# Level masks built later, and the input scaled by a product with a diagonal, in a hybrid HGRN2 / SSD / ConvFFN block

## The chip, the cores and the metric

The kernel runs on one core of a Trainium2 chip. Five engines work side by side, each through its own queue in order: TensorE (PE in the profile, PEld its weight loads), VectorE (DVE), ScalarE (ACT), GpSimd (POOL) and SyncE (SP), which issues most of the loads. They wait for each other by semaphores. The metric is the device time of one execution in microseconds (us), lower is better.

## What is computed

One layer on 512 tokens of width 2048, all in float32. Cut to what matters here:

```python
mod = silu(c) @ w_mod + b_mod                      # 6 parts of 2048
h = rms_norm(x, norm1_w) * (1.0 + scale1) + shift1
proj = h @ w_in                                    # q, f, i, g | z, xbc, dt
o_a = hgrn2_mixer(q_h, f_h, i_h, g_h, ...)         # 8 heads, chunks of 64
o_b = ssd_mixer(z_s, xbc_s, dt_s, ...)             # 4 groups of 4 heads
x = x + gate1 * (concat(o_a, o_b) @ w_out)
h = rms_norm(x, norm2_w) * (1.0 + scale2) + shift2
u = causal_dwconv(h @ ffn_w_up, ...)
x = x + gate2 * ((silu(u_gate) * u_val) @ ffn_w_down)
out = rms_norm(x, final_norm_w)
```

The change touches two places: how `x` is divided by its root mean square and turned (features on the partitions), and when the masks of the HGRN2 mixer are made.

## The kernel before

Every large product is done as three products of rounded parts (L166 to L168): a weight chunk `raw` is loaded (L146, 256 rows by up to 512 columns), ACT rounds it to `whi` (L161), DVE makes the rest `wlo = raw - whi` (L162), and the activations are held in the same way as `hhi` and `hlo`. There are five buffers for `raw`, two for each of `whi` and `wlo`.

**The start.** Four tiles of 128 tokens of `x` are loaded. For each, `x_rstd` squares and sums on ACT (L303), makes the mean (L306) and takes the power -0.5 on POOL (L307). `x_norm` scales the tile on ACT (L310), turns its 16 blocks of 128x128 on PE (L278), four to a bank, and evicts the four banks to `xT`: three by ACT (L282), one by DVE (L284). Meanwhile DVE sums the modulation `silu(c) @ w_mod`: `mod_pair` takes eight loads `m` of 256 rows (L231; they share the five `raw` buffers) and adds 16 rows' products into `macc` (L236, L238). Eight pairs are needed; each gives two blocks of `modT` (L246 to L249), with which `make_h1` makes `hhi` and `hlo` of two blocks (L329 to L331). So the weight products start when pair 0 and `xT` are there.

**The order of the work.** The SSD columns of `w_in` come first, in segments of a few blocks of rows (`SEGMENTS`), as the pairs become ready; between them stands the first value group, `v_group(0)`. A scheduler orders the instructions of each engine by the order of the program, with some work raised in priority; what stands in a queue is then fixed.

**The masks.** HGRN2 works with seven levels of blocks. `level_masks` writes ones to `one8` (DVE, L668) and cuts seven masks of 128x256 bytes out of it by two selects each on POOL (L672, L674), 14 in all. Before, it stands ahead of the segments. The masks are first read in `hgrn_mix`, after `v_group(1)`.

**The SSD mixers.** After the segments, `ssd_mix` of two groups at a time runs in small steps between the products of `v_group(1)` (`small`). Its helper `decay` fetches a table `mm` of head decays by a DMA that POOL issues (L434: one row for all 128 partitions, 256 KB), and DVE adds (L437), clips (L439) and, behind an exponential on ACT (L440), multiplies it (L441). PE turns blocks of `xbc` into small banks `mis` (L449), which DVE reads for `xdt` (L455) and `y` (L456). The pool of `mis` has two banks, so a turn waits until DVE has read the bank of two turns ago.

Of the kernel before, what the change touches and what calls it, by code (L numbers as in the profile page):

```python
# [10 lines left out]
AF = mybir.ActivationFunctionType  # L11
ALU = mybir.AluOpType
PSUM = bass.MemoryType.PSUM

P = 128
S = 512
NT = S // P
# [17 lines left out]
def hybrid_block_kernel(  # L35
# [22 lines left out]
    def nm(s):  # L58
        uid[0] += 1
        return f"{s}_{uid[0]}"  # L60

    def E(dtype=F32, name="e", tag="e"):
        return big.tile([P, 2048], dtype, tag=tag, name=nm(name), bufs={"e": 13, "y": 2, "a": 2}[tag])

    def T(name="t", dtype=F32):
        return tmp.tile([P, 512], dtype, tag="t", name=nm(name))
# [3 lines left out]
    def ACC(name="acc"):  # L70
        if wide[0]:
            wide[0] += 1
            if wide[0] % 8 in (0, 1):
                return MIS(name)
        return psa.tile([P, 512], F32, tag="acc", name=nm(name))

    def MIS(name="mis"):
        return psm.tile([P, 512], F32, tag="mis", name=nm(name))

    def SM(cols, name="s"):  # L80
        return sml.tile([P, cols], F32, tag=f"s{cols}", name=nm(name))

    def CT(shape, name, dtype=F32):
        return cst.tile(shape, dtype, tag=name, name=name)

    V, A, G, PE = nc.vector, nc.scalar, nc.gpsimd, nc.tensor
# [5 lines left out]
    ident = CT([P, P], "ident")  # L92
# [19 lines left out]
    def vec_rows(parts, name, q=nc.gpsimd):  # L112
        rows = T(name + "r")
        r = 0
        for ap, k in parts:
            q.dma_start(out=rows[r:r + k, 0:P], in_=ap)
            r += k
        return rows, r, name
# [8 lines left out]
    def r1(ap):  # L127
        return ap.rearrange("o (r p) -> (o r) p", p=P)
# [143 lines left out]
                      start=True, stop=True)  # L272
        return ps

    def transposed_one(src, dst, k0, t, evac, ps, n=4):

        for j in range(n):
            PE.transpose(out=ps[:, j * P:(j + 1) * P], in_=src[:, (k0 + j) * P:(k0 + j + 1) * P], identity=ident)  # L278
        o = dst.rearrange("p (j s) -> p j s", j=4)[:, k0 % 4:k0 % 4 + n, t * P:(t + 1) * P]
        i = ps[:, 0:n * P].rearrange("p (j s) -> p j s", j=n)  # L280
        if evac % 2:
            A.copy(out=o, in_=i)  # L282
        else:
            V.tensor_copy(out=o, in_=i)  # L284

    def modulate(src, kt, rb, a, sh, hi, lo):
        t = T("hm")
        V.scalar_tensor_tensor(out=t, in0=src, scalar=a, in1=rb, op0=ALU.mult, op1=ALU.mult)
        A.activation(out=hi, in_=t, func=AF.Identity, bias=sh)
        V.scalar_tensor_tensor(out=lo, in0=t, scalar=sh, in1=hi.bitcast(F32), op0=ALU.add, op1=ALU.subtract)  # L290


    xs_ = [E(name="x") for _ in range(NT)]
    xT = [E(name="xT", tag="a" if q == 3 else "e") for q in range(4)]

    def x_load(t):
        nc.sync.dma_start(out=xs_[t], in_=xd[t * P:(t + 1) * P, :])

    xr = {}

    def x_rstd(t):
        ssq = SM(1, "ssq")
        A.activation(out=xbc[t].rearrange("p b s -> p (b s)"), in_=xs_[t], func=AF.Square, accum_out=ssq)  # L303
        ms = SM(1, "ms")
        xr[t] = r = SM(1, "rstd")
        A.activation(out=ms, in_=ssq, func=AF.Copy, scale=1.0 / D, bias=EPS)  # L306
        G.tensor_tensor(out=r, in0=ms, in1=expo[:, 0:1], op=ALU.pow)  # L307

    def x_norm(t):
        A.activation(out=xs_[t], in_=xs_[t], func=AF.Copy, scale=xr[t])  # L310
        for q in range(4):
            transposed_one(xs_[t], xT[q], 4 * q, t, q < 3, ACC())

    hhi = [None] * KT
    hlo = [None] * KT
# [195 lines left out]
    def ov(t):  # L511
        return otile[t // 2].rearrange("p (t f) -> p t f", t=2)[:, t % 2, :]
# [153 lines left out]
    def level_masks():  # L666
        one8 = tmp.tile([P, 256], I8, tag="t", name="one8")
        V.memset(one8, 1)  # L668
        for h in LEVELS:
            nb = P // (2 * h)  # L670
            m = CT([P, 256], f"lm{h}", I8)
            G.affine_select(out=m, in_=one8, pattern=[[0, 4], [-2 * h, nb], [0, h]], base=0,  # L672
                            channel_multiplier=1, compare_op=ALU.is_ge, fill=0.0)
            G.affine_select(out=m, in_=m, pattern=[[0, 4], [2 * h, nb], [0, h]], base=h - 1,  # L674
                            channel_multiplier=-1, compare_op=ALU.is_ge, fill=0.0)
            lmask[h] = m
# [16 lines left out]
    def advance(p, q=8):  # L693

        while steps and steps[0] <= (p, q):
            next(gens[steps.pop(0)[0]], None)

    for t in range(NT):
        x_load(t)
    rows_1 = vec_rows([(r1(b_mod), 96), (r1(norm1_w), 16), (r1(norm2_w), 16)], "p1", nc.sync)  # L700
    for t in range(NT):
        x_rstd(t)
        x_norm(t)
        advance(0, 2 * t + 1)
    p1 = vec_t(*rows_1)
# [1 line left out]
    advance(0, 8)  # L707
    rows_2 = vec_rows([(r1(hgrn_gnorm_w), 8), (r1(ssd_norm_w), 8), (r2(ssd_conv_w), 64), (r1(ssd_conv_b), 16),
                       (hgrn_lb.rearrange("l (r p) -> (l r) p", p=P), 16)], "p2")
    level_masks()  # L710
    seen = set()
    n_piece = 0
    def v_group(grp):
# [6 lines left out]
    for st, k0, k1 in SEGMENTS:  # L720
# [35 lines left out]
        for (_, blocks), ac in zip(sets[st], accs):  # L756
            for b_, a_ in zip(blocks, ac):
                src, d_ = (a_, dtraw) if b_ is None else (a_, xbc[b_[0]][:, b_[1], :])
# [7 lines left out]
            ssd_dt(dtraw)  # L766
        seen.add(st)

    for g in (0, 3, 2, 1):
        waiting.append(ssd_mix(g))  # L770
    v_group(1)
# [12 lines left out]
    for j in range(2):  # L784
# [11 lines left out]
        for t in range(NT):  # L796
            yo = yv(t)[:, j * 512:(j + 1) * 512]
            for i in range(2):
                V.tensor_scalar(out=yo[:, i * 256:(i + 1) * 256], in0=yo[:, i * 256:(i + 1) * 256],
                                scalar1=r[:, 2 * t + i:2 * t + i + 1], scalar2=None, op0=ALU.mult)  # L800
# [18 lines left out]
    for j in range(2):  # L819
# [5 lines left out]
        for t in range(NT):  # L825
            sg = T("gs")
            A.activation(out=sg, in_=accs[t], func=AF.Silu)
            for i in range(4):
                h = 4 * j + i
                o = ov(t)[:, h * P:(h + 1) * P]  # L830
                V.scalar_tensor_tensor(out=o, in0=o, scalar=orstd[:, h, t:t + 1], in1=sg[:, i * P:(i + 1) * P],
                                       op0=ALU.mult, op1=ALU.mult)
# [33 lines left out]
    for n in range(4):  # L866
        accs = feat_group([(512 * n, 512)], [bl(i) for i in range(4)], chunk_src=wout, kts=order[::2], span=(8, 8),
                          rhs=(mhi, mlo), kk_in=True)
        with tc.high_priority(offset=2000 if n == 3 else 0):
            for i in range(4):  # L870
                kt = 4 * n + i
                V.scalar_tensor_tensor(out=x1f(kt), in0=accs[i], scalar=modT[:, 64 + kt:65 + kt], in1=x1f(kt),
                                       op0=ALU.mult, op1=ALU.add)
# [11 lines left out]
    with tc.high_priority(offset=2000):  # L885
        ps = MIS()
# [16 lines left out]
    for i in range(3):  # L903
        rows = T("fr")
        nc.scalar.dma_start(out=rows[0:2 * NF, 0:P], in_=fw[i * 2 * NF:(i + 1) * 2 * NF, :])
        ps = MIS()
# [4 lines left out]
    ps = MIS()  # L911
# [126 lines left out]
```

## Time and profile before

| what | us |
|---|---|
| median of 3 runs | 2513.89 |
| lowest and highest | 2510.45, 2513.9 |
| the profiled execution: its time | 2516.08 |
| the profiled execution: its span | 2514.4 |
| PE busy in the span | 2443.9 |
| DVE busy in the span | 1497.7 |
| mean granted clock of PE | 0.988 |

A row of the timeline reads: start and duration in us, engine, line, operation, what is written `<-` what is read, shape and count, and in brackets the idle time of the engine before it and what ended it. A row of the waits reads: who waits `<-` for whom, us in total, times, longest. A row of a stretch reads: start:end, its length, busy us of PE, PEld, DVE, ACT and POOL with counts, the granted PE clock, the DMA share and GB/s. Names are the program's, buffer numbers left out. The load bandwidth by fortieths of the span shows where loads are dense: about 270 GB/s in the first three, about 110 behind them, and more again between about 0.57 and 1.2 ms.

### The profile page before, as it was taken

The page shows a single profiled execution, that of the slowest core. Times are in us where ns is not written, and L with a number is a line of the kernel's source. Part 1 is how long each engine was busy: PE and PEld are TensorE (multiplying, and loading weights), DVE is VectorE, ACT ScalarE, POOL GpSimd, SP SyncE. Part 2 cuts the span into 40 slices and gives each one's busy share as a digit, 9 for nine tenths or more (in the row PEclk, how much of TensorE's full clock was granted, in tenths as well). Part 3 has the DMA queues.
Part 4 walks back from the last instruction along what each step waited for, and adds up shares of the span by engine and source line. Part 5 has one row for each costly group of instructions (what it writes and reads, how often), then busy time and mean ns, then how long its engine had stood idle before and what let it go on. Part 6 is the DMA issues. An engine that isn't in the chain of part 4 may idle for free.

```text
span 2514.4 us, 29234 instructions
## 1 busy us (share of the span) xinstructions
PE 2443.9 (97%) x11287; PEld 2015.4 (80%) x11287; DVE 1497.7 (60%) x2253; ACT 754.8 (30%) x1035; POOL 54.1 (2%) x66
## 2 busy tenths in 40 slices
PE   6999998999999999999999999999999999999998
PEld 5777877788878777887888888888888888888887
DVE  6884866556767656587636363635454545454557
ACT  6323422221322432332222222222222222232323
POOL 4000000000000000000000000000000000000000
PEclk8999999999999999999999999999999999999999
DMA  8893575335455666466323332333323232323242
GB/s 272 263 280 107 113 125 106 96 109 151 144 159 155 235 198 200 140 203 230 98 95 98 95 101 93 100 94 99 97 96 101 92 101 93 101 93 100 96 130 85
DMA packets 262823, 335.87 MB, mean 134 GB/s; under 512 B 18092, under 2 KB 182524, under 8 KB 261404
## 3 DMA queue, kind: packets, MB, share of 16 engines
q1 hardware_dynamic: 260432, 327.42, 41.5%
q0 software_dynamic: 1568, 4.31, 2.3%
q10 hardware_dynamic: 684, 2.28, 0.3%
q8 instruction: 88, 1.44, 0.2%
q14 instruction: 51, 0.42, 0.0%
HBM read 329.72 MB, written 4.23 MB: 133 GB/s over the span
## 4 chain that ended last, share of the span: by engine, by line
PE 81%; DMA 9%; DVE 7%; ACT 2%; issue 1%; SPq 0%; POOL 0%; ACTq 0%; DVEq 0%; POOLq 0%
PE acc L166 26%; PE acc L168 25%; PE acc L167 25%; DMA m<-in_w_mod_dram 7%; DVE wlo L162 2%; PE mis L547 2%; DVE macc L189 1%; DVE macc L238 1%; DMA raw<-in_w_in_dram 1%; ACT whi L161 1%; DMA x<-in_x_dram 1%; DMA mm<-acrow 0%; PE mis L201 0%; PE mis L487 0%; POOL rstd L265 0%
## 5 line engine op out<-in xcount | busy, mean ns | idle before, releaser
L162 DVE TENSOR_TENSOR wlo<-raw,whi 128x1024 fp32r<-128x1024 f32 (+1 forms) x408 | 490.4, 1203 | 744.9 <-ACT whi L161 739.3
L161 ACT CAST whi<-raw 128x1024 fp32r<-128x1024 f32 (+2 forms) x416 | 424.3, 1021 | 1403.3 <-PE acc L167 596.5
L166 PE MATMUL acc<-hhi,whi 128*128 128x512 f32 x1920 | 770.0, 402 | 11.7 <-ACT whi L161 7.1
L168 PE MATMUL acc<-hhi,wlo 128*128 128x512 f32 x1920 | 751.6, 394 | 3.6 <-DVE wlo L162 3.4
L167 PE MATMUL acc<-hlo,whi 128*128 128x512 f32 x1920 | 753.0, 392 | 0.0
L166 PEld LDWEIGHTS acc<-hhi,whi 128*128 128x128 f32 x1920 | 362.9, 189 | 87.2 <-ACT whi L161 11.2
L168 PEld LDWEIGHTS acc<-hhi,wlo 128*128 128x128 f32 x1920 | 362.4, 189 | 83.1 <-DVE wlo L162 6.5
L167 PEld LDWEIGHTS acc<-hlo,whi 128*128 128x128 f32 x1920 | 363.3, 189 | 67.9 <-issue 0.2
L166 PE MATMUL acc<-whi,act 128*128 128x512 f32 x640 | 249.0, 389 | 0.0
L167 PE MATMUL acc<-wlo,act 128*128 128x512 f32 x640 | 249.0, 389 | 0.0
L168 PE MATMUL acc<-whi,act 128*128 128x512 f32 x640 | 249.0, 389 | 0.0
L189 DVE SCALAR_TENSOR_TENSOR macc<-m,cT,macc 128x512 f32<-128x512 f32 x240 | 179.9, 750 | 106.8 <-DMA m<-in_w_mod_dram 102.6
L166 PE MATMUL acc<-whi,hhi 128*128 128x512 f32 x384 | 168.6, 439 | 0.0
L168 PE MATMUL acc<-whi,hlo 128*128 128x512 f32 x384 | 154.8, 404 | 0.0
L167 PE MATMUL acc<-wlo,hhi 128*128 128x512 f32 x384 | 154.0, 401 | 0.0
L166 PEld LDWEIGHTS acc<-whi,act 128*128 128x128 f32 x640 | 120.1, 188 | 25.0
L168 PEld LDWEIGHTS acc<-whi,act 128*128 128x128 f32 x640 | 120.1, 188 | 25.0
L167 PEld LDWEIGHTS acc<-wlo,act 128*128 128x128 f32 x640 | 120.1, 188 | 24.9
L950 DVE TENSOR_TENSOR g<-acc,gate 128x512 f32<-128x512 f32 x160 | 105.2, 683 | 3.9
L166 PE MATMUL acc<-mhi,whi 128*128 128x512 f32 x256 | 105.2, 411 | 0.0
L547 PEld LDWEIGHTS mis<-q,FK 128*128 128x128 f32 x448 | 83.5, 191 | 27.1 <-issue 8.3
L951 DVE TENSOR_TENSOR x<-x,g 128x512 f32<-128x512 f32 x160 | 105.1, 682 | 0.0
(263 smaller groups left out, 2249.8 us busy)
## 6 DMA issues: line engine op xcount, KB each, us to landing
raw<-in_ffn_w_up_dram SPq DMA_DIRECT2D x352, 256.0 KB, 2.9
m<-in_w_mod_dram SPq DMA_DIRECT2D x128, 512.0 KB, 4.3
raw<-in_ffn_w_down_dram SPq DMA_DIRECT2D x88, 512.0 KB, 3.6
m<-in_w_mod_dram SPq DMA_DIRECT2D x128, 256.0 KB, 4.3
raw<-in_w_in_dram SPq DMA_DIRECT2D x96, 256.0 KB, 3.5
raw<-in_w_in_dram SPq DMA_DIRECT2D x48, 512.0 KB, 3.8
raw<-in_w_out_dram SPq DMA_DIRECT2D x32, 512.0 KB, 4.6
x<-in_x_dram SPq DMA_DIRECT2D x8, 1024.0 KB, 10.6
```

What stands on the lines that cost most here:

```text
L161: A.copy(out=h_, in_=r_)
L162: V.tensor_tensor(out=l_, in0=r_, in1=h_.bitcast(F32), op=ALU.subtract)
L166: PE.matmul(out=ps, lhsT=lh, rhs=rh, start=first, stop=False)
L167: PE.matmul(out=ps, lhsT=lh, rhs=rl, start=False, stop=False)
L168: PE.matmul(out=ps, lhsT=ll, rhs=rh, start=False, stop=last)
L189: V.scalar_tensor_tensor(out=acc, in0=last[:, k, :], scalar=cT[:, kt:kt + 1], in1=acc, op0=ALU.mult, op1=ALU.add)
L238: V.scalar_tensor_tensor(out=acc, in0=m[:, k, :], scalar=cT[:, kt:kt + 1], in1=acc, op0=ALU.mult, op1=ALU.add)
L547: PE.matmul(out=ps[:, cch * 64:(cch + 1) * 64], lhsT=k[:, cch * P:(cch + 1) * P], rhs=qv[:, cch * npc:(cch + 1) * npc, 1, :], start=True, ...
L950: V.tensor_tensor(out=m, in0=accs[t], in1=gates[5][:, cs], op=ALU.mult)
L951: V.tensor_tensor(out=x1[t][:, cs], in0=x1[t][:, cs], in1=m, op=ALU.add)
```

## The change

`level_masks()` is called after the loop over the segments, ahead of the SSD mixers. `x_norm` no longer scales the tile: DVE multiplies the identity by the tile's norms, a diagonal `dg`, and PE multiplies each block with it, so that scaling and turning are one float32 product. Two of the four banks are evicted by DVE and two by ACT. `x_rstd` of a tile is written one tile ahead of `x_norm`.

```diff
     def x_norm(t):
-        A.activation(out=xs_[t], in_=xs_[t], func=AF.Copy, scale=xr[t])
+
+        dg = T("dg")[:, 0:P]
+        V.tensor_scalar(out=dg, in0=ident, scalar1=xr[t], scalar2=None, op0=ALU.mult)
         for q in range(4):
-            transposed_one(xs_[t], xT[q], 4 * q, t, q < 3, ACC())
+            ps = ACC()
+            for j in range(4):
+                PE.matmul(out=ps[:, j * P:(j + 1) * P], lhsT=xs_[t][:, (4 * q + j) * P:(4 * q + j + 1) * P], rhs=dg,
+                          start=True, stop=True)
+            o = xT[q].rearrange("p (j s) -> p j s", j=4)[:, :, t * P:(t + 1) * P]
+            i = ps.rearrange("p (j s) -> p j s", j=4)
+            if q % 2:
+                A.copy(out=o, in_=i)
+            else:
+                V.tensor_copy(out=o, in_=i)
...
     rows_1 = vec_rows([(r1(b_mod), 96), (r1(norm1_w), 16), (r1(norm2_w), 16)], "p1", nc.sync)
+    x_rstd(0)
     for t in range(NT):
-        x_rstd(t)
+        if t < NT - 1:
+            x_rstd(t + 1)
         x_norm(t)
         advance(0, 2 * t + 1)
...
-    level_masks()
     seen = set()
...
         seen.add(st)
 
+    level_masks()
     for g in (0, 3, 2, 1):
         waiting.append(ssd_mix(g))
```

The helper `transposed_one` goes with it. Line numbers behind it move: L310 of before has no successor, L303 becomes L292, the products are L305, the diagonal L301, the evictions L310 (ACT) and L312 (DVE).

At the start, DVE's queue before, from the first eviction of `xT` on (the rows on `macc` are the modulation sums of pair 0 over the loads `m`):

```order
L284 COPY xT_116<-acc_163 128x4x128
L236 TENSOR_SCALAR macc_169<-m_170,cT 128x512
L124 COPY p_305<-mis_303 128x128
L238 SCALAR_TENSOR_TENSOR macc_169<-m_170,cT,macc_169 128x512
L238 SCALAR_TENSOR_TENSOR macc_169<-m_175,cT,macc_169 128x512 x2
```

The same queue now, from the first diagonal to a few sums on:

```order
L301 TENSOR_SCALAR dg_150<-ident,rstd_141 128x128
L301 TENSOR_SCALAR dg_193<-ident,rstd_147 128x128
L312 COPY xT_113<-acc_152 128x4x128
L312 COPY xT_115<-acc_164 128x4x128
L236 TENSOR_SCALAR macc_176<-m_177,cT 128x512
L238 SCALAR_TENSOR_TENSOR macc_176<-m_177,cT,macc_176 128x512
L312 COPY xT_113<-acc_195 128x4x128
L238 SCALAR_TENSOR_TENSOR macc_176<-m_182,cT,macc_176 128x512
L301 TENSOR_SCALAR dg_235<-ident,rstd_190 128x128
```

Evictions and diagonals of the later tiles now stand between the sums. In this way six evictions and two diagonals, and both `wlo` of the first weight chunks, come behind the first sum and ahead of pair 0's last one, where two evictions stood.

POOL's queue before, behind the masks and the loads of the head parameters; `mm_2495` and `mm_2508` are the first decay tables of the two groups that run together:

```order
L399 DMA acrow<-acr_2035 64x128
L434 DMA mm_2495<-acrow 128x4x128
L434 DMA mm_2508<-acrow 128x4x128
L434 DMA mm_2694<-acrow 128x4x128
L434 DMA mm_2707<-acrow 128x4x128
```

POOL's queue now, the last eight of the 13 selects that stand between those two tables, which are `mm_2499` (ahead of the first select) and `mm_2512`:

```order
L672 AFFINE_SELECT lm_2428<-one_2417 128x256
L674 AFFINE_SELECT lm_2425<-lm_2425 128x256
L674 AFFINE_SELECT lm_2428<-lm_2428 128x256
L672 AFFINE_SELECT lm_2431<-one_2417 128x256
L672 AFFINE_SELECT lm_2434<-one_2417 128x256
L674 AFFINE_SELECT lm_2431<-lm_2431 128x256
L674 AFFINE_SELECT lm_2434<-lm_2434 128x256
L672 AFFINE_SELECT lm_2437<-one_2417 128x256
L434 DMA mm_2512<-acrow 128x4x128
L674 AFFINE_SELECT lm_2437<-lm_2437 128x256
L434 DMA mm_2698<-acrow 128x4x128
L434 DMA mm_2711<-acrow 128x4x128
```

The DMA of the second table has moved from right behind the first one to behind 13 selects.

DVE's queue now at the memset that the selects wait for (the rows are the end of the convolutions and the first steps of the two mixers; `wlo` is a weight chunk of `v_group(1)`):

```order
L763 TENSOR_TENSOR xbc_126<-xbc_126,acc_2272 128x512
L668 MEMSET one_2417 128x256
L427 TENSOR_TENSOR cbm_2497<-mis_2456,tri 128x512
L351 SCALAR_TENSOR_TENSOR cy_2411<-xbc_126,p_644,cy_2411 128x511
L427 TENSOR_TENSOR cbm_2510<-mis_2462,tri 128x512
L351 SCALAR_TENSOR_TENSOR cy_2411<-xbc_126,p_644,cy_2411 128x510
L455 TENSOR_TENSOR xdt_2455<-mis_2505,dtt 128x512
L162 TENSOR_TENSOR wlo_2638<-raw_2636,whi_2637 128x1024
L351 SCALAR_TENSOR_TENSOR cy_2411<-xbc_126,p_644,cy_2411 128x509
L437 TENSOR_TENSOR mm_2499<-mm_2499,negb 128x512
L456 TENSOR_TENSOR y_2453<-mis_2505,dskip 128x2x256
L439 TENSOR_SCALAR mm_2499<-mm_2499 128x512
```

and right behind it, from the add on the second table:

```order
L437 TENSOR_TENSOR mm_2512<-mm_2512,negb 128x512
L458 TENSOR_TENSOR xdt_2455<-xdt_2455,e_123 128x512
L439 TENSOR_SCALAR mm_2512<-mm_2512 128x512
L455 TENSOR_TENSOR xdt_2461<-mis_2518,dtt 128x512
L441 TENSOR_TENSOR mm_2499<-mm_2499,cbm_2497 128x512
L456 TENSOR_TENSOR y_2453<-mis_2518,dskip 128x2x256
L162 TENSOR_TENSOR wlo_2682<-raw_2680,whi_2681 128x1024
```

Without the memset these rows stood before in nearly the same order; the add on the second table was there too. `y_2453<-mis_2518` is the last reader of the bank that PE's next turn but one, `mis_2564`, takes over. PE's queue now around that turn, in the chunk of `whi_2637`:

```order
L166 MATMUL acc_2442<-whi_2637,hhi_1128 128x512
L167 MATMUL acc_2442<-wlo_2638,hhi_1128 128x512
L168 MATMUL acc_2442<-whi_2637,hlo_1129 128x512
L449 MATMUL mis_2564<-ident,xbc_128 128x128 x4
L166 MATMUL acc_2443<-whi_2637,hhi_1128 128x512
```

The turn now stands behind nine products of its chunk, before behind fifteen.

More of the change, by code (lines that the diff above doesn't have):

```diff
@@ L273, in rstd_bcast @@
         return ps
[L275 to L284, printed above, removed]
     def modulate(src, kt, rb, a, sh, hi, lo):
```

## The prediction

> **What bounds the kernel now.** I read the page first, then the waits, and then the two stretches that the change touches, in order of time.
>
> ```profile
> PE 2443.9 (97%) x11287; PEld 2015.4 (80%) x11287; DVE 1497.7 (60%) x2253; ACT 754.8 (30%) x1035; POOL 54.1 (2%) x66
> PE 81%; DMA 9%; DVE 7%; ACT 2%; issue 1%; SPq 0%; POOL 0%; ACTq 0%; DVEq 0%; POOLq 0%
> ```
>
> TensorE (PE) sets the end: busy for 97% of the span, 81% of the chain that ended last. So an edit counts only by what it does to PE's waits. The rest of the chain is mostly loads and VectorE (DVE). These are PE's waits from 36 to 200 us (first fence, where the first groups of weights and the modulation sums run) and its longest sum from 250 to 470 us (second fence, where the first SSD head groups run under the second value group).
>
> ```profile
> PE acc L166 <- ACT whi L161: 4.5, 3, 2.2
> PE acc L168 <- DVE wlo L162: 3.4, 5, 2.0
> PE acc L166 <- ACT hhi L330: 2.9, 1, 2.9
> PE mis L244 <- DVE macc L238: 1.2, 1, 1.2
> ```
>
> ```profile
> PE mis L497 <- DVE y L492: 11.8, 3, 4.4
> ```
>
> The first four add up to 12.0 us: that is all that any edit of the start can take from PE before 200 us, beside what it does to the first product.
>
> **Term A, the masks leave the start.** The masks take 14 selects on GpSimd (POOL), from 34.70 to 51.98 us. Grouped rows of DVE follow: from 34.5 to 53.6 us, beside them, and from 53.6 to 190 us, without them (count, busy us, mean ns).
>
> ```profile
> L238 DVE SCALAR_TENSOR_TENSOR macc<-m,cT,macc 128x512 f32<-128x512 f32 x14 | 14.6, 1043 | 0.4
> ```
>
> ```profile
> L238 DVE SCALAR_TENSOR_TENSOR macc<-m,cT,macc 128x512 f32<-128x512 f32 x91 | 68.0, 749 | 9.1 <-DMA m<-in_w_mod_dram 7.5
> ```
>
> The same sum takes 1043 ns beside the selects and 749 ns alone: 14 x 0.294 = 4.1 us of DVE time go. [...]
>
> What PE has of it: the wait of 2.0 us for wlo at 48.34, and the slow clock behind it.
>
> ```profile
> 48.34 0.50 PE L168 MATMUL acc<-hhi,wlo 128*128 128x512 f32 x1 [2.01 <-DVE wlo L162]
> ```
>
> ```profile
> 50.00:55.00 5.00, 5.00 (x19) 4.02 (x18) 4.01 (x6) 1.56 (x3) 3.57 (x6) 0.69 0.88 233
> ```
>
> A granted clock of 0.69 over 5 us loses 1.5 us. A is -3.5 us. Its bounds are 0 (later waits are for loads, and take it back) and -5.6 (all 4.1 us of DVE time carry through, and the clock).
>
> **Term B, the input's norm and turn.** The four scalings (2.0 us each) leave ScalarE (ACT); four small diagonals and four more evictions come to DVE; turns become products.
>
> ```profile
> 9.01 2.00 ACT L310 ACTIVATE x<-x,rstd 128x2048 f32<-128x2048 f32 x1 [0.66 <-POOL rstd L307]
> 11.07 3.67 PE L278 MATMUL acc<-ident,x 128*128 128x128 f32 x16 [8.26 <-ACT x L310]
> 14.78 0.69 DVE L284 COPY xT<-acc 128x512 f32<-128x512 f32 x1 [11.30 <-PE acc L278]
> ...
> 15.87 0.28 DVE L124 COPY p<-mis 128x128 f32<-128x128 f32 x1
> ...
> 30.34 0.16 DVE L247 SCALAR_TENSOR_TENSOR modT<-modT,p 128x2 f32<-128x2 f32 x1
> ...
> 31.01 1.97 PE L278 MATMUL acc<-ident,x 128*128 128x128 f32 x16 [0.90 <-ACT x L310]
> ...
> 31.93 1.82 DVE L162 TENSOR_TENSOR wlo<-raw,whi 128x1024 fp32r<-128x1024 f32 x2 [0.23 <-DMA m<-in_w_mod_dram]
> ...
> 33.74 1.54 ACT L329 ACTIVATE hm<-xT,modT 128x512 f32<-128x512 f32 x2
> ...
> 35.84 1.90 PE L166 MATMUL acc<-hhi,whi 128*128 128x512 f32 x4 [2.86 <-ACT hhi L330]
> ```
>
> ```profile
> L853 PE MATMUL mis<-ident,x x64: 270/271/329, 864.3 to 914.4; 128*128 128x128 f32 x64
> L570 PE MATMUL mis<-v,Kt x48: 270/274/377, 529.0 to 809.2; 128*128 128x128 f32 x48
> ```
>
> The 64 turns of L853 (16 blocks by 4 tiles) stand as 64 records, the 24 products of L570 (8 heads by 3 chunks) as 48: a turn is one pass and a float32 product two. So each input tile is 32 passes instead of 16: 3.9 us on the fast clock (1.97 / 16 = 0.123 each), 7.3 us on the slow one (3.67 / 16). PE is idle there. The first diagonal can be ready near 9.3 us, with no scaling ahead of it, and the squares no longer stand behind scalings, so one slow tile and three fast ones (19.0 us) can be through by about 28 us: the products hide. What is late next is DVE. In the changed order six evictions (0.69 each), two diagonals (about 0.25, by the 0.28 of a 128x128 copy) and both wlo of the first weights stand ahead of the last sums of pair 0, where two evictions stood: 2.8 + 0.5 + 1.8 = 5.1 us more. Pair 0's modulation was ready at 30.5 us and then waited for ACT until 33.74; the first weight product came 2.1 us after that. Now it is ready at 35.6, ACT is free, and the product comes at 37.7: B is +1.8 us. Bounds: -3.2 (ready as early as before, and ACT at once), and +3.5 (the late evictions and a diagonal also hold back the buffers of the loads, 1.7 us).
>
> **Term C, the masks at their new place.** Here lies the weight. The selects now stand on POOL's queue between the first table of head decays (L434, mm) and the second, 13 of 14 ahead of it. The second table's DMA cannot be issued until they are done. On DVE the add on it (L437) stands ahead of six steps, of which the last frees the bank that PE's next turn (L449) needs, since the pool for these has two banks. PE is in order too, so it stands.
>
> ```profile
> 307.20 0.68 DVE L762 TENSOR_TENSOR xbc<-xbc,acc 128x512 f32<-128x512 f32 x1
> 307.80 1.28 DVE L427 TENSOR_TENSOR cbm<-mis,tri 128x512 f32<-128x512 f32 x2
> ...
> 313.92 0.68 DVE L437 TENSOR_TENSOR mm<-mm,negb 128x512 f32<-128x512 f32 x1
> 314.52 0.68 DVE L456 TENSOR_TENSOR y<-mis,dskip 128x512 f32<-128x512 f32 x1
> ```
>
> ```profile
> 296.28 0.76 POOL L434 DMA_DIRECT2D mm<-acrow  x1 [7.84 <-PE mis L423]
> ```
>
> The sixteen such DMAs, from issue to landing:
>
> ```profile
> DMA to landing us min/median/max: 8.3/9.3/12.4
> ```
>
> The memset ahead of the selects, and selects of before (start, us):
>
> ```profile
> 34.35 0.27 DVE L668 MEMSET one<- 128x256 int8 x1
> ```
>
> ```profile
> 1.57 0.29 POOL L103 TENSOR_SCALAR_AFFINE_SELECT suf<-ones 128x128 f32<-128x128 f32 x1
> ...
> 34.70 4.18 POOL L672 TENSOR_SCALAR_AFFINE_SELECT lm<-one 128x256 int8<-128x256 int8 x2 [4.73 <-DVE one L668]
> ...
> 46.36 2.24 POOL L672 TENSOR_SCALAR_AFFINE_SELECT lm<-one 128x256 int8<-128x256 int8 x2
> ...
> 51.24 0.77 POOL L674 TENSOR_SCALAR_AFFINE_SELECT lm<-lm 128x256 int8<-128x256 int8 x1
> ```
>
> PE's chunk around that turn:
>
> ```profile
> 316.51 0.40 PE L166 MATMUL acc<-whi,hhi 128*128 128x512 f32 x1
> ...
> 318.59 0.39 PE L166 MATMUL acc<-whi,hhi 128*128 128x512 f32 x1
> ...
> 319.95 0.61 PE L449 MATMUL mis<-ident,xbc 128*128 128x128 f32 x4
> ```
>
> In times of before: the memset that the selects wait for comes between the first two rows, at 307.8 + 0.27 = 308.1. 13 selects are 51.24 - 34.70 = 16.5 us. The DMA then lands 8.5 us later (between least and median; the queue is quiet, as weight loads wait for DVE): 333.1. Six steps, each 0.6 after the last (313.92 to 314.52) and the one-input step L439 about half of that, are 3.3 us: 336.4. PE comes to that turn after nine products of its chunk instead of fifteen, at 318.6. It waits 17.8 us. Before, the same table was issued at 296.28 and had landed long before DVE asked at 313.92: this cover is what goes. C is +17.8. The least is 13 x 0.29 (the select of 128x128 at 1.57 us) = 3.8 us of selects and a landing of 8.3: a wait of 4.9. The most is the same selects with a landing of 12.4: 21.7. Selects of 2.1 us throughout, as in the first pair, are left out: the later pairs, beside the same busy DVE, took about half.
>
> [...]
>
> **Term D, the cold clock behind the wait.** After the longest L497 wait (4.4 us, ending near 349) the clock was 0.83 for 10 us: 1.7 us. After a longer one it is the same: D is +1.7 (0 to 2).
>
> ```profile
> 350.00:360.00 10.00, 10.00 (x46) 8.37 (x45) 6.64 (x16) 2.20 (x3) 0.75 (x1) 0.83 0.61 160
> ```
>
> **The sum.** -3.5 + 1.8 + 17.8 + 1.7 = +17.8 us on the profiled execution's 2516.1: 2533.9. That execution lay 2.2 us above the median of the runs, so I say 2531 us. A measurement of this kernel can tell about 0.2% (5 us) from no change: faster is below 2508.9, slower above 2518.9.
>
> **The rivals.**
>
> - Later waits take part of it back. The next wait of PE, at 345 us, hangs on a load that was slow among the tables:
>
> ```profile
> 335.58 8.57 DMA m<-in_w_mod_dram
> ...
> 437.94 8.63 DMA mm<-acrow
> ```
>
> ```profile
> m<-in_w_mod_dram SPq DMA_DIRECT2D x128, 512.0 KB, 4.3
> ```
>
> The tables behind the second one go out while PE stands, so this load could take the median of its kind, 4.3 us, and one more of the waits for L492 could shrink as much: 4 to 8 us back, 2523 to 2527. Against it: the load is itself issued behind DVE's wlo, which shifts with the rest.
>
> - The selects are quick, because DVE stands for most of them. At the fastest one's 0.77 us they take 10.0, the wait is 11.3, and the time 2525; at 0.29 the wait is 4.9 and the time 2519. Against it: no select took less than 0.77 in the row of before, and the first ones 2.1. [...]
>
> - Faster: the start carries all the way. If A is -5.6 and B is -3.2, PE is 8.8 us ahead at 200 us; with D at 0 the time is 2513.9 - 8.8 = 2505.1 plus C. It is faster by over 0.2% where C is below 3.8 us: selects of under 0.29 us each, with the best of both other terms. For it speaks only that every one of PE's first four waits hangs on DVE or ACT, whose work shrinks.
>
> - It does not do what it says: if the masks slowed DVE at the new place as at the old, with no table behind them, 4.1 us of DVE time would only move, to a stretch where 11.8 us of waits stand instead of 12.0: 2512 to 2516, no change. The order on POOL's queue speaks against it.
>
> **Chances.** The forecast (2526 to 2540) 0.58; part taken back, 0.18, slower as well; quick selects 0.12, of which 0.03 end within 0.2%; only moved, 0.04, within; faster 0.06; longer than 2540, 0.02. Slower 0.87, the same 0.07, faster 0.06. For 8 in 10 the range need not go to the last cases: 2517 (quick selects with a good start) to 2540 us (landing of 12.4, later start).
>
> **What would show it.** Right: on POOL 13 selects of together 10 to 17 us ahead of the second mm DMA; on DVE one wait of over 10 us at L437 for that DMA; on PE one wait of 11 to 20 us at a turn of L449 near 320 us; the macc sums near 40 us at 750 ns; the first weight product between 33 and 40 us. Wrong: the L449 wait under 5 us, or PE ahead by over 6 us at 300, or the waits behind 340 us gone.

## The result

The changed kernel takes 2528.78 us (median of 4 runs, 2527.85 to 2532.29) against 2513.89 us (2510.45 to 2516.95) before: the ratio is 1.0062, with a 95% interval of 1.0045 to 1.0080, so 11 to 20 us more. The profiled executions are 2527.85 us (span 2526.1) after and 2516.08 us (span 2514.4) before.

The page of the changed kernel, busy time by engine and the chain that ended last:

```profile
PE 2445.4 (97%) x11351; PEld 2018.4 (80%) x11351; DVE 1499.9 (59%) x2261; ACT 745.4 (30%) x1027; POOL 50.8 (2%) x66
PE 81%; DMA 8%; DVE 7%; issue 1%; ACT 1%; POOL 1%; SPq 0%; DVEq 0%; ACTq 0%; POOLq 0%
```

Nothing in the totals says where 12 us went: PE is busy for 1.5 us more than before. It is the waits that show it. The two largest of PE's waits from 250 to 480 us after the change (total, count, longest, us):

```profile
PE mis L449 <- DVE y L456: 13.1, 2, 11.2
PE mis L497 <- DVE y L492: 11.3, 3, 4.0
```

The second row stood there before, with 11.8 us. The first is new. It is followed back on three engines. POOL around the selects (start, us, what, and in brackets the idle time before it):

```profile
291.24 0.79 POOL L434 DMA_DIRECT2D mm<-acrow  x1 [30.88 <-ACT xbc L353]
306.90 3.35 POOL L672 TENSOR_SCALAR_AFFINE_SELECT lm<-one 128x256 int8<-128x256 int8 x2 [14.87 <-DVE one L668]
310.21 3.96 POOL L674 TENSOR_SCALAR_AFFINE_SELECT lm<-lm 128x256 int8<-128x256 int8 x2
...
319.44 0.46 POOL L672 TENSOR_SCALAR_AFFINE_SELECT lm<-one 128x256 int8<-128x256 int8 x1
319.85 0.78 POOL L434 DMA_DIRECT2D mm<-acrow  x1
```

POOL has nothing to do for 14.87 us, until DVE's memset is done; then 13 selects run for 12.95 us, and the second table of head decays is issued at 319.85. That is 28.6 us after the first table, where it was 8.6 us before (287.64 and 296.28). Of the 20.0 us more, 13.0 are the selects and 7.0 the longer idle time ahead of them (14.87 us for the memset; before, POOL stood 7.84 us ahead of this DMA). So the place of the memset in DVE's queue counts as well as the selects. DVE:

```profile
306.55 0.27 DVE L668 MEMSET one<- 128x256 int8 x1
...
307.43 1.58 DVE L351 SCALAR_TENSOR_TENSOR cy<-xbc,p,cy 128x511 f32<-128x511 f32 x1
...
310.44 0.68 DVE L455 TENSOR_TENSOR xdt<-mis,dtt 128x512 f32<-128x512 f32 x1
311.04 2.00 DVE L162 TENSOR_TENSOR wlo<-raw,whi 128x1024 fp32r<-128x1024 f32 x1
...
327.85 0.69 DVE L437 TENSOR_TENSOR mm<-mm,negb 128x512 f32<-128x512 f32 x1 [10.63 <-DMA mm<-acrow]
...
330.60 0.69 DVE L456 TENSOR_TENSOR y<-mis,dskip 128x512 f32<-128x512 f32 x1
```

DVE stands for 10.63 us at the add on that table, which lands 8.0 us after its issue. Ahead of that wait its steps are long as well, but not all: the wlo takes 2.00 us and the step of the convolution (L351) 1.58, where rows of before have 1.23 and 0.74; the xdt keeps its 0.68. The y that frees PE's bank ends at 331.29. PE:

```profile
316.33 0.63 PE L449 MATMUL mis<-ident,xbc 128*128 128x128 f32 x4 [1.83 <-DVE y L456]
...
331.43 1.09 PE L449 MATMUL mis<-ident,xbc 128*128 128x128 f32 x4 [11.25 <-DVE y L456]
...
337.92 0.60 PE L462 MATMUL mis<-ident,xbc 128*128 128x128 f32 x4
```

Three waits for DVE stand in a row, 0.69 (at 309.76), 1.83 and 11.25 us, 13.8 us together; before, no turn of L449 in this stretch waited. The L462 at the end of the stretch is the one that began at 322.02 before.

The start, in PE's waits from 36 to 200 us, and the macc sums of DVE from 36 to 55 us (count, then busy us, mean ns):

```profile
PE acc L166 <- ACT whi L161: 5.0, 3, 2.9
PE acc L166 <- ACT hhi L330: 2.5, 1, 2.5
PE mis L244 <- DVE macc L238: 1.3, 2, 1.0
PE acc L168 <- DVE wlo L162: 0.5, 1, 0.5
```

```profile
L238 DVE SCALAR_TENSOR_TENSOR macc<-m,cT,macc 128x512 f32<-128x512 f32 x14 | 10.5, 751 | 0.9 <-DMA m<-in_w_mod_dram 0.6
```

The sums went from 1043 to 751 ns, and the wait for wlo from 3.4 to 0.5 us. The first weight product came later:

```profile
34.02 1.87 PE L244 MATMUL mis<-ones,macc 128*128 128x1 f32 x8 [6.60 <-DVE macc L238]
```

```profile
36.12 0.16 DVE L247 SCALAR_TENSOR_TENSOR modT<-modT,p 128x2 f32<-128x2 f32 x1
```

```profile
38.39 1.22 PE L166 MATMUL acc<-hhi,whi 128*128 128x512 f32 x2 [2.51 <-ACT hhi L330]
```

That is 38.39 instead of 35.84 us. With these points each kernel can be cut into three: to the first weight product, to the turn of dtraw (L365) behind the start, and from there to the L462 behind the selects.

### The profile page after: what moved, and what is told of

It reads as the page before. It is cut to its first block, busy times and chain, and to the rows that moved or that the text cites. A ratio compares the mean times of both kernels' runs of the same rounds, so it can differ in the third digit from the quotient of the medians.

```text
span 2526.1 us, 29368 instructions
## 1 busy us (share of the span) xinstructions
PE 2445.4 (97%) x11351; PEld 2018.4 (80%) x11351; DVE 1499.9 (59%) x2261; ACT 745.4 (30%) x1027; POOL 50.8 (2%) x66
## 4 chain that ended last, share of the span: by engine, by line
PE 81%; DMA 8%; DVE 7%; issue 1%; ACT 1%; POOL 1%; SPq 0%; DVEq 0%; ACTq 0%; POOLq 0%
PE acc L166 26%; PE acc L168 25%; PE acc L167 25%; DMA m<-in_w_mod_dram 6%; DVE wlo L162 2%; PE mis L547 2%; DVE macc L189 1%; DVE macc L238 1%; DMA mm<-acrow 1%; ACT whi L161 1%; PE acc L305 1%; DMA x<-in_x_dram 0%; DMA raw<-in_w_in_dram 0%; DVE xbc L763 0%; DMA raw<-in_ffn_w_up_dram 0%
## 5 line engine op out<-in xcount | busy, mean ns | idle before, releaser
L166 PEld LDWEIGHTS acc<-hhi,whi 128*128 128x128 f32 x1920 | 362.9, 189 | 88.4 <-ACT whi L161 12.4
```

Of the source, the lines that this page charges most:

```text
L166: PE.matmul(out=ps, lhsT=lh, rhs=rh, start=first, stop=False)
```

## The experiments

Each kernel ran on one chip with the kernel before, and the medians of the kernel before in these rows differ by up to 3 us (2510.88 to 2513.89), so kernels of different rows are set against each other by their ratios. The table has the median, that of the kernel before beside it, the ratio with its 95% interval, and from the profiled execution the start of the first weight product, that of L365, and the time from L365 to the first L462 (us; the last is what term C and D are about):

| kernel | median | before | ratio | first product | L365 | L365 to L462 |
|---|---|---|---|---|---|---|
| before | 2513.89 | | | 35.84 | 245.68 | 76.34 |
| changed | 2528.78 | 2513.89 | 1.0062 (1.0045 to 1.0080) | 38.39 | 244.42 | 93.50 |
| e1, masks moved only | 2526.90 | 2511.86 | 1.0049 (1.0036 to 1.0062) | 34.78 | 242.29 | 93.89 |
| e2, turn only | 2514.97 | 2511.86 | 1.0013 (1.0005 to 1.0022) | 38.46 | 248.46 | 76.35 |
| e3, second table by SP | 2518.93 | 2511.86 | 1.0026 (1.0017 to 1.0036) | 38.26 | 242.61 | 82.89 |
| e4, masks first | 2517.72 | 2511.86 | 1.0023 (1.0014 to 1.0032) | 44.24 | 253.03 | 76.34 |
| e5, masks in a gap, old turn | 2507.66 | 2511.05 | 0.9988 (0.9979 to 0.9997) | 35.98 | 244.19 | 76.33 |
| e6, masks in a gap, new turn | 2512.71 | 2511.05 | 1.0007 (0.9998 to 1.0015) | 38.40 | 245.30 | 76.34 |
| e7, e6 with evictions on ACT | 2510.71 | 2511.05 | 0.9994 (0.9985 to 1.0003) | 34.88 | 244.48 | 76.36 |
| e8, three levels late | 2516.95 | 2510.88 | 1.0026 (1.0015 to 1.0038) | 38.28 | 242.51 | 83.42 |

In e4 the L365 and L462 of the table bear the numbers 380 and 477, in e3 L462 is 463. The last column repeats to 0.03 us in all six kernels without late selects; the column L365 does not (the changed kernel and e3 do the same work up to there, and stand 1.8 us apart), so a difference of 2 us there means nothing in one execution. The first product lies within 0.2 us in five kernels with the new turn (changed, e2, e3, e6 and e8: 38.26 to 38.46), but only within 1.2 us in the three with the old one (34.78 to 35.98).

**e1, the masks alone moved.**

```
@@ before
-    level_masks()
     seen = set()
...
+    level_masks()
     for g in (0, 3, 2, 1):
         waiting.append(ssd_mix(g))
```

> The kernel before with the level masks alone moved behind the segments; the norm and turn of the input stay as before. If the wait for the second table of head decays makes the loss, and the new turn adds its 2.5 us of later first weight product on top: 2526 us (2524 to 2528), with one wait of PE of 10 to 13 us at the turn L449 near 320 us, and the first weight product at 35.8 us. Rival, the new turn costs nothing by the end: the time of the changed kernel, 2529 us (2528 to 2531). Rival, the new turn is what costs: 2510 to 2514 us.

Measured: ratio 1.0049, 12.3 us (9 to 16), and 17.6 us more than before from L365 to L462. The first weight product came at 34.78. One long wait stands at L449:

```profile
329.81 1.09 PE L449 MATMUL mis<-ident,xbc 128*128 128x128 f32 x4 [11.70 <-DVE y L456]
```

The move of the masks makes most of the loss; that the turn is what costs is out. How much the turn adds to it can't be read here: by the ratios the changed kernel lies 3.3 us higher (0.0013), with intervals that overlap, and by the medians, each less its own before, 14.9 against 15.0 us, it lies no higher.

**e2, the new turn alone.** It is the changed kernel with level_masks() back at its old line.

> The changed kernel with the masks back at their old place, so only the norm and turn of the input are changed. If the later first weight product (38.4 instead of 35.8 us) carries through to the end: 2516.5 us (2515 to 2518), no wait above 3 us at L449. Rival, it is absorbed by later waits for loads: 2513 to 2515 us. Rival, the turn costs nearly as much as the masks: above 2520 us.

Measured: ratio 1.0013, 3.3 us (1.3 to 5.5). From L365 to L462 it is like before (76.35). As a time, 2514.97 lies at the rival's 2513 to 2515, but the kernel before was faster on this chip (2511.86), and the ratio counts. The turn costs about what the later first product says, 2.6 us; that later waits absorb all of it is out, that they absorb a part is not.

**e3, one DMA on another queue.** The selects stay at the new place.

```
@@ changed kernel, decay
-            nc.gpsimd.dma_start(out=m.rearrange("p (c t) -> p c t", c=4),
+            q = nc.sync if (g, h) == (3, 0) else nc.gpsimd
+            q.dma_start(out=m.rearrange("p (c t) -> p c t", c=4),
```

> The changed kernel, in which one DMA alone, the table of the first decay of the second head group, is issued from SP's queue instead of POOL's; the selects stay where they are. If the wait is for POOL's queue: the wait at L437 goes, the wait at L449 near 320 falls from 11.3 to under 3 us, and the time is 2513 to 2519 us. The later tables, still behind the selects, land near 329 us and are asked for after 330. Rival, the selects cost by slowing DVE beside them (steps of 0.6 us took 1.1 to 2.0 us there): the wait at L449 keeps 5 us or more, and the time stays above 2522 us.

Measured: ratio 1.0026, 9.1 us less than the changed kernel by the ratios (0.0036 of 2514). DVE (the added line moves the numbers by one):

```profile
309.23 2.00 DVE L162 TENSOR_TENSOR wlo<-raw,whi 128x1024 fp32r<-128x1024 f32 x1
311.15 1.48 DVE L351 SCALAR_TENSOR_TENSOR cy<-xbc,p,cy 128x509 f32<-128x509 f32 x1
...
314.32 1.20 DVE L438 TENSOR_TENSOR mm<-mm,negb 128x512 f32<-128x512 f32 x1 [0.54 <-DMA mm<-acrow]
...
316.87 0.67 DVE L457 TENSOR_TENSOR y<-mis,dskip 128x512 f32<-128x512 f32 x1
```

and PE:

```profile
317.69 0.63 PE L450 MATMUL mis<-ident,xbc 128*128 128x128 f32 x4 [3.87 <-DVE y L457]
```

The wait for the table is gone (10.63 to 0.54 us), and so is PE's wait of 11.25. But 3.87 us are left at the turn before it. DVE's steps beside the selects are still long, and the order has changed with the edit: the add on the second table now stands ahead of the y that this turn waits for, and stood behind it in the changed kernel (there the turn waited 1.83 us). The time is at the upper end of the first expectation, and the wait that is left between the two. The last column splits the loss: of 17.2 us (93.50 - 76.34), 10.6 go with POOL's queue (93.50 - 82.89), and 6.6 are left with the selects beside DVE, each with the slow products behind its wait (0.63 us each, from 332.74 on in the changed kernel and from 319.15 on in e3, against 0.39 to 0.47 behind the same turn in the kernel before). The queue's block without selects beside DVE was not tried, so this split takes for DVE's share what e3 leaves, the changed order included.

**e4, the masks before the input arrives.** level_masks() stands right behind the constants of the changed kernel.

> The changed kernel with the masks built among the constants, before the input arrives, where DVE has little to do. If a select takes 0.45 us when DVE stands: 14 of them take 6 to 7 us, from about 2 to 9 us, the first norm's power on POOL is hardly later, and the time is 2510 to 2514 us: nothing of the masks at the later places, and the later first product of the new turn left. Rival, a select of 128x256 takes 0.77 us or more also beside an idle DVE: they end after 12 us, hold up the first norm by 3 us or more, and the time is 2515 to 2519 us.

Measured: ratio 1.0023, 5.8 us slower than before; the first expectation falls. POOL:

```profile
1.85 3.35 POOL L120 TENSOR_SCALAR_AFFINE_SELECT lm<-one 128x256 int8<-128x256 int8 x2
5.16 3.36 POOL L122 TENSOR_SCALAR_AFFINE_SELECT lm<-lm 128x256 int8<-128x256 int8 x2
8.47 1.51 POOL L120 TENSOR_SCALAR_AFFINE_SELECT lm<-one 128x256 int8<-128x256 int8 x2
9.93 1.51 POOL L122 TENSOR_SCALAR_AFFINE_SELECT lm<-lm 128x256 int8<-128x256 int8 x2
11.38 0.93 POOL L120 TENSOR_SCALAR_AFFINE_SELECT lm<-one 128x256 int8<-128x256 int8 x2
12.27 0.93 POOL L122 TENSOR_SCALAR_AFFINE_SELECT lm<-lm 128x256 int8<-128x256 int8 x2
13.14 0.47 POOL L120 TENSOR_SCALAR_AFFINE_SELECT lm<-one 128x256 int8<-128x256 int8 x1
...
14.12 0.55 POOL L311 TENSOR_TENSOR rstd<-ms,expo 128x1 f32<-128x1 f32 x1
```

From 6.9 to 14.7 us DVE does nothing here. Still the pair of levels 4 and 8 takes 1.51 us and that of 16 and 32 only 0.93: a select's time hangs on its level, not only on DVE. The 0.46 us that the expectation took from the standing DVE of the changed kernel belonged to the levels that came last. All 14 end at 14.1 us, the first norm waits for them (14.12 instead of 8.29 us), and the first weight product comes at 44.24.

**e5, the masks in a gap, with the old turn.** DVE has few steps from 198 to 235 us, and POOL none.

```
@@ before
-    level_masks()
     seen = set()
...
         if st is None:
             v_group(0)
+            level_masks()
             continue
```

> The kernel before with the masks built right behind the first value group, so that the selects run from about 190 us, where DVE has few steps from 198 to 235 us and no table of decays stands behind them. The norm and turn of the input are those of before. If the selects at the start really cost what their end gives back (term A, 3.5 us) and cost nothing at 190: the time is 2.5 to 4.5 us below the kernel before on the same chip (ratio 0.998 to 0.999), and the last hlo near 190 us are 0.3 to 1 us longer each. Rival, later waits for loads take the gain back before 200 us: within 1 us of the kernel before. Rival, the hlo beside the selects come late for the last products of the value group: 1 to 4 us slower than before.

Measured: ratio 0.9988, 3.0 us faster (0.8 to 5.3). The selects ran from 192.79 us; no later table stood right behind them (76.33 from L365 to L462). This is term A by itself, and the lowest ratio of the study, below the kernel before and the changed one. Two of PE's waits from 36 to 200 us, and the stretch from 46 to 56 us, before and here:

```profile
PE acc L166 <- ACT whi L161: 4.5, 3, 2.2
PE acc L168 <- DVE wlo L162: 3.4, 5, 2.0
46.00:56.00 10.00, 7.99 (x32) 6.28 (x31) 8.34 (x13) 2.61 (x6) 7.57 (x10) 0.83 0.84 236
```

```profile
PE acc L166 <- ACT whi L161: 6.1, 5, 2.3
PE acc L168 <- DVE wlo L162: 1.4, 2, 1.1
46.00:56.00 10.00, 9.68 (x46) 7.32 (x44) 7.46 (x15) 5.93 (x10) 0.00 (x0) 1.00 0.88 259
```

The wait for wlo fell by 2.0 us, and the granted clock rose from 0.83 to 1.00 over 10 us (1.7 us at most), as term A has it. The waits for whi grew by 1.6 us, so part of the gain was taken back.

**e6, the same with the new turn.** It has the line of e5 in the changed kernel.

> The changed kernel with the masks built right behind the first value group, as in the run with the old turn. If the new turn costs its 2.5 to 3 us also without selects behind it: 2.5 to 3.5 us above the run with the old turn, about the time of the kernel before (ratio 0.9990 to 1.0005), the first weight product at 38.4 us. Rival, the turn costs only because it pushes the sums of the next pairs into the selects at 38 to 55 us: the same as the run with the old turn within 1 us.

Measured: ratio 1.0007; 4.8 us above e5 by the ratios (more than the 2.5 to 3.5 expected), the intervals do not meet, and a first product at 38.40. The turn costs also where no select follows it; the rival falls.

**e7, e6 with the evictions on ACT.**

```
-            if q % 2:
+            if q < 3:
                 A.copy(out=o, in_=i)
```

> As the run before it, but three of the four evictions of each turned tile are on ACT, as in the kernel before, and one on DVE; products and diagonals stay. If the evictions on DVE delay the last sums of pair 0 (term B, 8 evictions of 0.69 us against 4): the first weight product comes at 35.5 to 37 us instead of 38.4, and the time is 1 to 3 us below the run before it. Rival, the products in two passes, or the clock of 0.51 behind the idle start, set that point: the first weight product stays at 38 us or later. Rival, ACT with its squares and twelve evictions becomes the late engine: the first weight product at 39 us or later.

Measured: modT of pair 0 was ready at 32.7 us instead of 36.3, and PE's first product came 3.5 us earlier:

```profile
34.88 1.22 PE L166 MATMUL acc<-hhi,whi 128*128 128x512 f32 x2 [3.38 <-ACT hhi L330]
```

That is earlier than the 35.5 to 37 us expected. So it is the evictions on DVE that delay it, not the products in two passes; ACT had room for them. With them DVE's order changed too: pair 0's last sum is done at 29.96 us, ahead of both `wlo` (at 30.62), which stand ahead of it in e6 (30.43, the last sum ends near 34.0). So the 3.5 us are the four evictions and this change of order together. In the time, 0.9994 against 1.0007 for e6 leans the same way (3 us), with intervals that meet; against e5 (0.9988) nothing is told apart.

**e8, three levels late.** Levels 1, 2, 4 and 8 are built in the gap, and 16, 32 and 64 at the new place, so 5 selects stand ahead of the second table.

```
-    def level_masks():
+    def level_masks(levels):
...
             v_group(0)
+            level_masks(LEVELS[:4])
...
-    level_masks()
+    level_masks(LEVELS[4:])
     for g in (0, 3, 2, 1):
```

> The changed kernel with the masks of the levels 1, 2, 4 and 8 built behind the first value group and only those of 16, 32 and 64 at the new place: 5 selects instead of 13 stand ahead of the second table. If POOL's queue makes the wait, one for one: 5 selects of 0.46 us are 2.3 us instead of 13, the table lands 8 to 9 us behind them, 10.3 to 11.3 us after the memset instead of 21, the wait of DVE at L437 falls from 10.6 to 2 to 4.5 us, that of PE at L449 near 320 from 11.3 to under 4, and the time is 2 to 5 us above the run with all masks behind the value group (ratio to before 1.0013 to 1.0027). Rival, any select at that place costs the whole wait, since the landing is what counts: the waits stay over 8 us, ratio 1.0045 or more. Rival, the few selects hide under the steps of DVE that come first: no wait at L437 for the table, ratio below 1.0012.

Measured: ratio 1.0026. POOL, DVE and PE:

```profile
304.99 0.92 POOL L672 TENSOR_SCALAR_AFFINE_SELECT lm<-one 128x256 int8<-128x256 int8 x2 [14.86 <-DVE one L668]
305.87 1.36 POOL L674 TENSOR_SCALAR_AFFINE_SELECT lm<-lm 128x256 int8<-128x256 int8 x2
307.17 0.90 POOL L672 TENSOR_SCALAR_AFFINE_SELECT lm<-one 128x256 int8<-128x256 int8 x1
308.02 0.78 POOL L434 DMA_DIRECT2D mm<-acrow  x1
```

```profile
316.28 0.69 DVE L437 TENSOR_TENSOR mm<-mm,negb 128x512 f32<-128x512 f32 x1 [5.19 <-DMA mm<-acrow]
```

```profile
318.39 1.09 PE L449 MATMUL mis<-ident,xbc 128*128 128x128 f32 x4 [5.32 <-DVE y L456]
```

The issue came 9.9 us sooner behind the memset (3.1 instead of 13.0 us), and the landing took 8.3 us instead of 8.0. DVE's wait fell by 5.4 us only (10.63 to 5.19): DVE, less slowed by selects (its wlo took 1.39 us instead of 2.00) and with two steps fewer ahead of the add (the y and L439 now stand behind it), also came to it 4.2 us sooner. The waits are somewhat over those of the first expectation, the time is within it. A few short selects are enough: 3.2 us of them go with a loss of 7.1 us from L365 to L462. Most of that is not their own length: POOL stands 14.86 us for the memset ahead of them, so the second table is issued 18.7 us after the first (289.33 and 308.02) instead of 8.6, and its landing of 8.3 us no longer hides. An earlier memset, at which the selects would run in that idle time, was not tried.

## Why the prediction was right

- **The path of the loss (term C) was right, and e3 and e8 show it.** Selects ahead of the table on POOL, DVE at L437, the bank of the turn, PE at L449. The pieces, from the end of the memset (306.82): issue after 13.0 us where 16.5 was said, landing 8.0 (8.5), DVE's steps 3.4 (3.3), and PE's own arrival at the turn 13.4 us after the memset (331.43 - 11.25) where 10.5 was said.
- **Its size was too large.** PE's waits are 13.8 us, not 17.8. The step that failed: I took the selects' length from the row of before, where DVE was busy all through, and held the short ones at the end for a matter of DVE alone. e4 shows that the level sets most of it: 13 selects with DVE mostly idle are 12.1 us (3.35 + 3.36 + 1.51 + 1.51 + 0.93 + 0.93 + 0.47). So the bound of 3.8 us from a select of 128x128 was no bound for these, and the rival of quick selects had nearly the right wait for a wrong reason. That it came so near (11.3 and 11.25 us) is luck. PE's arrival is the other error: it was delayed by 2.5 us of shorter waits, as DVE's steps beside the selects grew. The sum put this slowing of DVE at the new place at nothing; in e3, with the queue out of the way, 6.6 us are left from L365 to L462.
- **The cold clock (term D) was too small**: 1.7 us said, 2.8 measured. Before, the turn and 7 products stood from 319.95 to 322.02; after, the turn and 14 products took 331.43 to 337.92. The 14 took 5.75 us; at the pace of before (1.70 us for the first seven, 0.23 for each more) they would have taken 3.3. That is 2.4 us, and 0.4 on the turn. Three of the products, and the granted clock over the stretch:

```profile
332.74 0.63 PE L167 MATMUL acc<-wlo,hhi 128*128 128x512 f32 x1
337.00 0.61 PE L168 MATMUL acc<-whi,hlo 128*128 128x512 f32 x1
337.69 0.39 PE L167 MATMUL acc<-wlo,hhi 128*128 128x512 f32 x1
```

```profile
331.40:337.90 6.50, 6.47 (x18) 5.23 (x19) 5.81 (x9) 0.00 (x0) 0.00 (x0) 0.53 0.29 83
```

  I had taken 0.83 from the stretch behind the wait that ends at 349.27, averaged over 10 us. That wait is 3.87 us long, not 4.4 (the one of 4.4 us ends at 433.60), and behind it the products of 0.63 us are over by 353.3. "After a longer one it is the same" is the step of term D that failed: behind 11.25 us the slow products go on for 5.3 us (332.17 to 337.43), or 6.0 with the turn. The granted clock was 0.50 from 332.1 to 337.4 us and 1.00 from 337.4 to 345; behind the wait of 3.87 us in the kernel before it was 0.60 from 349.27 to 353.3 and 0.98 from there to 360. What sets how long the slow products go on was not shown. C and D together are 13.8 + 2.8 and 0.6 us of unnamed gaps: 17.2 us in the last column of the table, 19.5 in the prediction.
- **Term A was right in size, and its path is shown in part**: -3.5 us said, -3.0 (-5.3 to -0.8) in e5. The sums took 751 ns in the changed kernel, and the wait for wlo fell, by 2.9 us there and by 2.0 us in e5, where the clock gave up to 1.7 us as well. But e5's four waits from 36 to 200 us add up to 12.1 us, as much as before (12.0), since those for whi and macc grew; how much of the 3 us each piece carries to the end is open.
- **Term B was right in its mechanism, and small**: first product 37.7 said, 38.39 measured; 3.3 us (1.3 to 5.5) in e2 and 4.8 between e5 and e6, where 1.8 was said. DVE's part of it is shown by e7. The two diagonals, the six evictions and the wlo came ahead of the last sum as said; what was missed is that PE's eight small products on that sum ran for 1.87 us behind 6.60 us of idle, at a granted clock of 0.50 from 34.0 to 35.9 us (before, 1.03 us with none), so modT was ready at 36.3 instead of 35.6. The 2.1 us from there to the product were exact.
- **The sum.** -3.0 + 3.3 + 17.2 = 17.5 us by the runs' parts, 15.6 (11 to 20) measured by the ratio, 17.8 predicted on the profiled execution. C was 4.0 us too large; B (1.5 us), D (1.1), A (0.5) and the unnamed gaps (0.6) made up for nearly all of it. That the sum came so close is luck; that its largest term was the wait at L449, and rightly traced, is not. Part taken back later, as the first rival had it, was not seen where that rival put it: the waits for L492 are 11.3 us instead of 11.8, not 4 to 8 less. The profiled execution shows 15.9 us at L462 and 11.7 at the end; the stretch from the first product on `Kt` (L570) to the first turn of the reloaded x (L853, there L855) took 332.8 us in the changed kernel and 335.3 before, but 333.0 in e2 and 335.1 in e8, so it goes with neither the selects nor the turn, and no cause was found in the change.
- The rivals that end faster or without a change are out: the order on POOL's queue did bite.

## What to carry to other kernels

On POOL's queue, which here computes and also issues DMAs, the computation ahead of a DMA became part of the time until its data were there (13.0 us of selects, and the idle time in which they waited for their own input). Before work is moved onto such a queue, look for the next DMA behind it, for the engine that stands at it in order, and for what the moved work itself waits for. Work with nothing waiting for it belongs where its engine is idle and no transfer stands behind it, and not only where its result is needed late: here a gap 110 us earlier turned a loss of 12 us (e1) into a gain of 3 (e5). A duration taken from a row with a mean or a merged count should be split by what differs in it, here the level, before it is used as a price or as a bound.

## What the runs showed of the hardware

- A select on a 128x256 int8 tile took longer the shorter the blocks of its mask. In e4 the pairs took 3.35 us (blocks of 1 and 2 columns), 1.51 (4 and 8) and 0.93 (16 and 32), the last single one 0.47 (64).
- Not every DVE step took longer beside a select. In the changed kernel the wlo (two inputs in SBUF) went from 1.23 to 2.00 us, the sums of the convolution from 0.74 to 1.58, the one-input L439 from 0.42 to 1.11; the cbm and xdt beside them, with one input from a PSUM bank, kept their 0.68. What makes the difference was not shown. In e4 a copy of 64x64 took 2.10 us beside the first select, from 1.92 to 4.02 us, where it took 0.19 in the kernel before, ahead of any select of a mask:

```profile
1.92 2.10 DVE L107 COPY l1m<-suf 64x64 f32<-64x64 f32 x1
4.03 1.22 DVE L108 TENSOR_SCALAR l1m<-tri 64x64 f32<-64x64 f32 x1
```

- The 256 KB table took 8.0 us to land from POOL's queue in the changed kernel, and 9.8 us from SP's queue (e3, issue at 304.48, DVE's wait for it over at 314.32). The sixteen from POOL's queue took 8.3 to 12.4 us in the kernel before, so this one does not tell the two queues apart.
